# RWKV-7 recurrence in a two-layer encoder: transitions formed ahead of the chain, scratch laid out by token tile, transfers merged and spread

## The chip, the cores and the metric

One core of a Trainium2 chip runs the whole program. The metric is the device time of one execution in microseconds (us); the program is timed as a whole. Engines: TensorE (PE; its weight loads are PEld), VectorE (DVE), ScalarE (ACT), GpSimd (POOL) and SyncE (SP), whose queue issues the DMAs named here. Each engine runs its own instructions in the order in which they stand.

## What is computed

A trunk of two layers on 1024 tokens of width 1024, in float32. Layer 0 is attention and an MLP, and the change leaves both alone. Layer 1 mixes tokens by an RWKV-7 recurrence with 16 heads of 64, once forward and once backward, and then has an MLP. What matters of it:

```
def rwkv7_scan(r, w, k, v, kk, a):
    def step(state, inp):
        r_t, w_t, k_t, v_t, kk_t, a_t = inp
        sa = jnp.einsum('bhvk,bhk->bhv', state, -kk_t)
        state = (state * w_t[:, :, None, :] + sa[..., None] * (kk_t * a_t)[:, :, None, :]
                 + v_t[..., None] * k_t[:, :, None, :])
        return state, jnp.einsum('bhvk,bhk->bhv', state, r_t)
...
    for d in range(2):
        ...
        o = rwkv7_scan(*ins)            # reversed in time for d == 1
        ...
        dir_out.append((group_norm(o, gn_w, gn_b) + bonus.reshape(nB, S, D)) * g.astype(F32))
    y = dir_out[0] + dir_out[1]
    return y.astype(h.dtype) @ w_o
```

## The kernel before

The program runs attention, its MLP, the RWKV projections (`rwkv_proj`), the recurrence (`rwkv_scan`), the output projection (`layer_out`) and the second MLP. A scheduler orders the instructions within what the code's order, the buffers and the data allow; `tc.high_priority` moves some forward, and `tc.issue_after` ties one behind another.

`rwkv_proj` makes r, k, v, the decays, the rates and the gates in pieces of 128 channels by 512 tokens, and writes them to scratch in DRAM: per group of four heads (256 channels, two pairs of heads) `dr.rk` (r and the normed key), `dr.v`, `dr.y` (the bonus) and `dr.g` (gates, one per direction), laid out as partition, pair, 1024 tokens; a piece is stored in runs of 2 KB. `dr.x` (decay sums, rates, keys) is laid out by tile already, with runs of about 512 bytes.

`rwkv_scan` cuts the sequence into chunks of 64 tokens. Its unit of work, a tile here, is 128 tokens (two chunks c) of four heads in both directions: 16 chunk problems. Four tiles make a batch; there are 8 batches, so 32 tiles G, and one step of the main loop per tile. Direction 1 walks the tokens backward, so tile e of a group pairs tokens e (forward) with tile 7 - e (backward). Per tile there are these generators:

- `prep` loads x and rk of each direction, raises the decays (ScalarE), forms scaled queries `zr` (VectorE, L1253 and L1255) and keys `bk` (VectorE L1260, POOL L1261), multiplies them on TensorE (L1267) to the intra-chunk matrices `af`, which ScalarE copies out (L1270) and POOL masks (L1271). TensorE transposes the keys (L1279), ScalarE copies them to `bn` (L1281). `bk` holds each head's half of the partitions with zeros in the other half, so TensorE always works on all 128 rows. The strictly triangular part goes to the scratch `nd`.
- `invert`, once a batch, loads `nd` as `nb`, inverts 32x32 blocks by 60 small VectorE operations (L1298, L1300), stores them to `xd` and loads them back into `af` and as `xt`. All these transfers stand together behind the last operation.
- `post` loads v, centres it (L1339) into `sv`, and joins the inverted blocks (TensorE L1353, L1364, ScalarE copies L1357, L1367).
- `scan` walks the chain: for each of two chunks, two pairs of heads and two directions, TensorE adds what the state h gives to the chunk (L1389, L1393), ScalarE and VectorE copy that to `y` (L1395, L1396), TensorE applies the inverse (L1398), both engines copy to `sv` (L1400, L1401), TensorE forms the state's increment (L1404), VectorE the new state (L1413, with ScalarE's decayed old one, L1387), and TensorE the output (L1419, L1424), which ScalarE copies out to `ot` (L1427). Behind each of these eight visits `side()` advances the other generators by one piece.
- `finish` norms the output (TensorE L1446, two matmul records per tile, counted below to find steps), gates it, adds the bonus (POOL L1456) and stores to `yh`, or with the second half of the sequence to `yd`, which the output projection reads (L748).

Nine slots hold prepared tiles, so `prep` runs eight tiles ahead of the chain. Four chains of state are open at a time (two pairs, two directions), and a chunk of one of them needs the state of its predecessor.

Of the kernel before, what the change touches and what calls it, by code (L numbers as in the profile page):

```python
# [842 lines left out]
def rwkv_proj(tc, g, ap, ru, dr):  # L843
# [6 lines left out]
    with ExitStack() as es:  # L850
# [83 lines left out]
        def quad(x, pr, half):  # L934
            return x[pr // 2][:, pr % 2, ..., fsl(half, 512)] if len(x[0].shape) == 3 else x[pr // 2][:, pr % 2, :, fsl(half, 512)]

        def r_done(half):
            def done(pr, ps):
                o = po.tile([P, 512], F32, tag="o", name="o")
                nc.scalar.activation(o, ps, AF.Copy)  # L940
                nc.sync.dma_start(out=quad(dr.rk, pr, half)[:, 0], in_=o)

            return done
# [10 lines left out]
        def v_done(half):  # L954
            def done(pr, ps):
                y = po.tile([P, 512], F32, tag="y", name="y")
                nc.sync.dma_start(out=y, in_=quad(yb, pr, half))
                o = po.tile([P, 512], F32, tag="o", name="o")
                nc.scalar.activation(o, ps, AF.Copy)
                nc.sync.dma_start(out=quad(dr.v, pr, half), in_=o)  # L960
                nc.gpsimd.tensor_tensor(out=y, in0=y, in1=o, op=ALU.mult)
                nc.sync.dma_start(out=quad(dr.y, pr, half), in_=y)
# [44 lines left out]
        class Side:  # L1007
# [22 lines left out]
            def norm(self, nh, pr):  # L1030
# [18 lines left out]
                nc.sync.dma_start(out=quad(dr.rk, pr, nh)[:, 1], in_=kk)  # L1049

            def unit(self, w, nh, pr, d):
# [5 lines left out]
                if d == 0:  # L1057
# [3 lines left out]
                    nc.sync.dma_start(out=w.r, in_=quad(dr.rk, pr, nh)[:, 0])  # L1061
# [29 lines left out]
                nc.sync.dma_start(out=quad(dr.g[d], pr, nh), in_=o)  # L1091
# [11 lines left out]
                if d == 1:  # L1103
                    nc.gpsimd.tensor_tensor(out=w.y, in0=w.y, in1=kr, op=ALU.add)
                    nc.sync.dma_start(out=quad(yb, pr, nh), in_=w.y)
# [39 lines left out]
def rwkv_scan(tc, g, ap, dr, yd):  # L1145
# [3 lines left out]

    nc = tc.nc  # L1150
    NS = T // P
    NX = 4 * (65 + 2 * RC)
    with ExitStack() as es:
# [13 lines left out]
        hp = pool("s_h", 3)  # L1167
# [3 lines left out]
        t1 = pool("s_1", 1, "left")  # L1171
        te = pool("s_e", 2, "left")
        ip = pool("s_i", 1, "left")
        slots("left", 0, 1, 2, 8)
        psC = pool("s_pc", 1, space=PSUM)
        psA = pool("s_pa", 2, space=PSUM)
        psB = pool("s_pb", 1, space=PSUM)
# [8 lines left out]
        nc.vector.memset(gneps, GN_EPS)  # L1186

        dp = es.enter_context(tc.tile_pool(name="s_d", bufs=2, space=DRAM))


        hbd = [[t1.tile([P, P], F32, name=f"h{d}{i}") for i in range(2)] for d in range(4)]
        ybd = [t1.tile([P, 2, RC], F32, name=f"y{d}") for d in range(4)]
        for x in sum(hbd, ybd):
            nc.gpsimd.memset(x, 0.0)
        bk = t1.tile([P, 4, 2, 2, RC], F32, name="bk")
        for j in range(2):
            nc.gpsimd.memset(bk[fsl(1 - j, 64), :, j], 0.0)
# [4 lines left out]
        def psb():  # L1202
            return psB.tile([P, 512], F32, tag="B", name="B", bufs=1)

        def psl():
            return psB.tile([P, 512], F32, tag="L", name="L", bufs=1)
# [4 lines left out]
        def tokens(d, e, n):  # L1211

            return slice(e * P, (e + n) * P) if d == 0 else slice((NS - e - n) * P, (NS - e) * P)
# [5 lines left out]
        def quad(x):  # L1219
            return x.rearrange("p (q c) t -> p q c t", q=2)  # L1220

# [10 lines left out]
        def prep(q, i):  # L1232
# [4 lines left out]
            w.af = sp.tile([P, 2, 4, 2, P], F32, tag="af", name="af")  # L1237
            w.zr, w.bn = ([sp.tile([P, 4, 2, RC], F32, tag=f"{n}{d}", name=f"{n}{d}") for d in range(2)] for n in ("zr", "bn"))
            w.pc = [sp.tile([P, 4], F32, tag=f"pc{d}", name=f"pc{d}") for d in range(2)]
            for d in range(2):  # L1240
                x = te.tile([P, NX], F32, tag="x", name="x")
                nc.sync.dma_start(out=x, in_=dr.x[d][q.m][:, e, :])
                rk = te.tile([P, 2, 2, P], F32, tag="rk", name="rk")
                nc.sync.dma_start(out=rk, in_=dr.rk[q.m][:, :, :, tokens(d, e, 1)])
# [3 lines left out]
                ipr = te.tile([P, 4, RC], F32, tag="ipr", name="ipr", bufs=1)  # L1248
                nc.scalar.activation(ipr, cs[:, :, 1:65], AF.Exp, scale=KAPPA)
                nc.scalar.activation(cs, cs, AF.Exp, scale=-KAPPA)  # L1250
                nc.gpsimd.tensor_copy(w.pc[d], cs[:, :, 64])
                zr = w.zr[d]
                nc.vector.tensor_tensor(out=quad(zr[:, :, 0]), in0=quad(cs[:, :, 0:64]), in1=ordered(rk[:, :, 1], d),  # L1253
                                        op=ALU.mult)
                nc.vector.tensor_tensor(out=quad(zr[:, :, 1]), in0=quad(cs[:, :, 1:65]), in1=ordered(rk[:, :, 0], d),  # L1255
                                        op=ALU.mult)

                for j in range(2):
                    rows = fsl(j, 64)
                    nc.vector.tensor_tensor(out=bk[rows, :, j, j], in0=kd[rows], in1=ipr[rows], op=ALU.mult)  # L1260
                    nc.gpsimd.tensor_tensor(out=bk[rows, :, j, 1 - j], in0=a[rows], in1=ipr[rows], op=ALU.mult)  # L1261
                yield

                for j in range(2):
                    ps = psa()
                    for u in range(4):
                        nc.tensor.matmul(ps[:, fsl(u, P)], lhsT=bk[:, u, j].rearrange("p a b -> p (a b)"),  # L1267
                                         rhs=zr[:, u].rearrange("p a b -> p (a b)"), start=True, stop=True)
                    o = w.af[:, d, :, j, :]
                    nc.scalar.activation(o, ps.rearrange("p (u t) -> p u t", t=P), AF.Copy)  # L1270
# [193 lines left out]
        class Bulk:  # L1464


            def __init__(self):
                self.l = []
# [233 lines left out]
```

## Time and profile before

| | us |
|---|---|
| three timed runs | 3662.55, 3665.97, 3673.72; median 3665.97 |
| the profiled execution | 3667.36 |
| its span | 3665.6 |
| first to last preparation product (L1267) | 1896.3 to 2706.5 |
| first to last output copy of the chain (L1427) | 2088.6 to 2863.0 |
| TensorE busy over the span | 3183.3 (87%) |
| VectorE, ScalarE, POOL busy | 2533.5, 1849.0, 1772.7 |

Times inside the execution count from the span's start. "Busy" is the time in which at least one instruction of the engine ran; the granted clock (PEclk) is the part of TensorE's full clock that it was given. In the groups, `128*64 128x64` is the part of TensorE's array in use (rows by columns) and the result; a matmul of 32-bit floats leaves two records, a transpose one; "idle before" names what the engine waited for ahead of the group. In the waits the columns are total us, times, and the longest.

### The profile page before, as it was taken

How to read it: one execution, taken by the hardware profiler on the slowest of the kernel's cores; microseconds unless marked ns; L12 is line 12 of the kernel's file. 1: busy time of each engine (PE TensorE's matmuls, PEld its weight loads, DVE VectorE, ACT ScalarE, POOL GpSimd, SP SyncE). 2: the span in 40 equal slices, each digit the busy share in tenths (PEclk: the TensorE clock that was granted, in tenths of full speed). 3: DMA queues.
4: the chain of work that ended last, by engine and by line, in shares of the span. 5: the costliest groups of instructions: out<-in, count | busy, mean ns of one | idle time of the engine just before them, and what ended most of it. 6: DMA issues, size and time to landing. Idle time of an engine off the chain costs nothing. (4 is left out here: it accounts for less than half of the span.)

```text
span 3665.6 us, 61287 instructions
## 1 busy us (share of the span) xinstructions
PE 3183.3 (87%) x22168; PEld 2592.9 (71%) x22168; DVE 2533.5 (69%) x4649; ACT 1849.0 (50%) x4244; POOL 1772.7 (48%) x1610
## 2 busy tenths in 40 slices
PE   7999998899999988888887687788777889999998
PEld 6788887688777766665566566666666768877776
DVE  3355564654499978966954778887776474449996
ACT  2366564455543337754433365565566445554333
POOL 1000001565598884354666344444431156558887
PEclk9999999899999998999986687788887889999999
DMA  6222215233231133258775354455444423223113
GB/s 202 72 79 81 67 55 176 84 128 115 75 126 50 66 113 111 92 177 230 229 226 157 92 129 111 106 128 124 114 100 132 129 78 141 109 70 138 37 79 115
DMA packets 425101, 425.70 MB, mean 116 GB/s; under 512 B 138668, under 2 KB 338476, under 8 KB 418653
## 3 DMA queue, kind: packets, MB, share of 16 engines
q1 hardware_dynamic: 423612, 417.58, 36.8%
q0 software_dynamic: 1184, 4.20, 0.4%
q8 instruction: 174, 2.85, 0.3%
q14 instruction: 131, 1.07, 0.1%
HBM read 290.83 MB, written 138.20 MB: 117 GB/s over the span
## 5 line engine op out<-in xcount | busy, mean ns | idle before, releaser
L101 PE MATMUL pm<-bhi,lo 128*128 128x512 f32 x840 | 332.7, 399 | 45.6 <-DVE lo L130 45.4
L130 DVE TENSOR_TENSOR lo<-x,hi 128x512 fp32r<-128x512 f32 x300 | 322.0, 1079 | 63.3 <-ACT hi L129 63.1
L129 ACT ACTIVATE hi<-x 128x512 fp32r<-128x512 f32 x300 | 189.2, 631 | 330.1 <-DVE x L127 128.9
L100 PE MATMUL pm<-blo,hi 128*128 128x512 f32 x840 | 331.5, 395 | 8.7 <-POOL blo L130 8.2
L99 PE MATMUL pm<-bhi,hi 128*128 128x512 f32 x840 | 320.9, 395 | 5.3 <-ACT bhi L129 5.3
L127 POOL TENSOR_TENSOR x<-w1r 128x512 f32<-128x512 f32 x160 | 214.5, 1344 | 201.6 <-DVE lo L130 178.2
L1271 POOL TENSOR_TENSOR af<-af,amask 128x512 f32<-128x512 f32 x128 | 164.6, 1291 | 146.1 <-ACT af L1270 103.8
L130 POOL TENSOR_TENSOR blo<-bx,bhi 128x512 fp32r<-128x512 f32 x138 | 222.8, 1615 | 25.3 <-ACT bhi L129 25.0
L1267 PE MATMUL A<-zr,bk 128*128 128x128 f32 x1024 | 187.5, 347 | 47.1 <-DVE bk L1260 36.1
L101 PEld LDWEIGHTS pm<-bhi,lo 128*128 128x128 f32 x840 | 158.3, 189 | 98.1 <-DVE lo L130 66.8
L905 POOL TENSOR_TENSOR wl<-wr,wh 128x512 fp32r<-128x512 f32 (+2 forms) x144 | 160.1, 1123 | 127.8 <-ACT wh L904 92.7
L127 POOL TENSOR_TENSOR bx<-w 128x512 f32<-128x512 f32 x140 | 215.9, 1544 | 9.5
L1267 PEld LDWEIGHTS A<-zr,bk 128*128 128x128 f32 x1024 | 166.5, 250 | 59.8 <-POOL bk L1261 22.1
L127 DVE TENSOR_TENSOR x<-h 128x512 f32<-128x512 f32 x140 | 195.9, 1410 | 5.3 <-ACT h L268 2.7
L100 PEld LDWEIGHTS pm<-blo,hi 128*128 128x128 f32 x840 | 158.8, 189 | 49.4 <-POOL blo L130 16.0
L99 PEld LDWEIGHTS pm<-bhi,hi 128*128 128x128 f32 x840 | 159.8, 191 | 39.0 <-ACT bhi L129 6.2
L99 PE MATMUL mm<-xmh,wh 128*128 128x512 f32 x384 | 166.6, 452 | 9.3 <-ACT wh L904 5.4
L1413 DVE SCALAR_TENSOR_TENSOR h<-c,pc,hd 64x64 f32<-64x64 f32 x448 | 127.0, 283 | 50.1 <-PE c L1404 30.6
L886 DVE SCALAR_TENSOR_TENSOR x<-u,mu,x 128x512 f32<-128x512 f32 x192 | 153.9, 834 | 9.2 <-ACT x L884 6.7
L1419 PE MATMUL c<-af,sv 128*64 128x64 f32 x1024 | 97.3, 274 | 72.3 <-DVE h L1413 65.4
L583 ACT ACTIVATE S<-S,mneg 128x256 f32<-128x256 f32 (+2 forms) x256 | 124.5, 499 | 67.8 <-DVE mneg L578 44.8
L335 DVE TENSOR_TENSOR acc<-acc,pm 128x512 f32<-128x512 f32 x256 | 158.1, 675 | 0.0
(369 smaller groups left out, 9951.2 us busy)
## 6 DMA issues: line engine op xcount, KB each, us to landing
w1r<-in_mlp_w_dram SPq DMA_DIRECT2D x32, 1024.0 KB, 5.5
w<-in_mlp_w_dram SPq DMA_DIRECT2D x32, 1024.0 KB, 5.4
x<-x SPq DMA_DIRECT2D x64, 386.0 KB, 3.3
hd<-h SPq DMA_DIRECT2D x24, 1024.0 KB, 4.2
h<-hd SPq DMA_DIRECT2D x24, 1024.0 KB, 7.8
wr<-in_w_rkv_dram SPq DMA_DIRECT2D x96, 256.0 KB, 2.7
rk<-rk SPq DMA_DIRECT2D x64, 256.0 KB, 3.9
x<-cs SPq DMA_DIRECT2D x32, 260.0 KB, 4.2
```

The lines of the kernel that those rows point to most:

```text
L99: nc.tensor.matmul(out, lhsT=ahi, rhs=bhi, start=start, stop=False)
L100: nc.tensor.matmul(out, lhsT=ahi, rhs=blo, start=False, stop=False)
L101: nc.tensor.matmul(out, lhsT=alo, rhs=bhi, start=False, stop=stop)
L127: add.tensor_tensor(out=y, in0=x, in1=blocks[term[2]], op=ALU.add if term[1] == "+" else ALU.subtract)
L129: nc.scalar.activation(hi, x, AF.Copy)
L130: sub.tensor_tensor(out=lo, in0=x, in1=hi, op=ALU.subtract)
L335: dve.tensor_tensor(out=a, in0=a, in1=banks[j], op=ALU.add if sign == "+" else ALU.subtract)
L886: nc.vector.scalar_tensor_tensor(out=x, in0=at(2 * i), scalar=mu[:, i, c, kt:kt + 1], in1=x, op0=ALU.mult, op1=ALU.add)
L905: nc.gpsimd.tensor_tensor(out=wlo, in0=wr, in1=whi, op=ALU.subtract)
L1267: nc.tensor.matmul(ps[:, fsl(u, P)], lhsT=bk[:, u, j].rearrange("p a b -> p (a b)"), rhs=zr[:, u].rearrange("p a b -> p (a b)"), start=Tru ...
L1271: nc.gpsimd.tensor_tensor(out=o, in0=o, in1=consts["amask"].unsqueeze(1).to_broadcast([P, 4, P]), op=ALU.mult)
L1413: nc.vector.scalar_tensor_tensor(out=hn[rows, cols], in0=ch[rows, 128:192], scalar=pc[rows, u:u + 1], in1=hd[rows, cols], op0=ALU.mult, op ...
```

## The change

The chain is rewritten so that it holds only the state. A new generator `post_a` does what `post` did and also multiplies the centred values by the intra-chunk matrix (`y`, L1396 of the new code). A new generator `post_b` applies the inverse to the queries and to that product (L1420), and from the first result forms, per chunk, the transition of the state and the effective queries (TensorE L1431, VectorE L1435 and L1437, where `eye2` is the identity twice). It then starts the sums for the new state (`hb`) and the output (`ob`) in PSUM, with the parts that don't need the state (L1406, in the helper `sums`). `scan` adds to these sums what the state gives, once per chunk for all eight problems (two pairs of heads, two directions, two heads in the halves of the partitions), and multiplies by the decay (VectorE L1467).

In `prep` the keys hold one head per half of the partitions without zeros, in one operation each (VectorE L1273, POOL L1274), and TensorE's products (L1282) work on 64 rows at a time, in turn the upper and the lower; the transposes (L1295) take 128 rows, and there is a new one of `zr` (L1303). `sv` has no zeros left to set.

The scratch `rk`, `v`, `y`, `g`, `yh` and `yd` is laid out as partition, token tile, pair, 128 tokens. `both(x, e)` addresses the tiles of both directions at once, so `rk`, `v`, `y` and the results have one transfer per tile in place of two. The stores of `rwkv_proj`, and its reload of r, keep their piece of 512 tokens and are cut to runs of 512 bytes.

`invert` sets the blocks' diagonal on VectorE in place of POOL and issues its loads tile by tile over several pieces, its stores behind the latest loads and key copies (`mark`). The main loop has a written table of which generator advances at which of eight places of a step; loads are issued one step before their use.

The core of the diff:

```
-            w.af = sp.tile([P, 2, 4, 2, P], F32, tag="af", name="af")
+            xs = [te.tile([P, NX], F32, tag="x", name="x", bufs=3) for d in range(2)]
             for d in range(2):
-                rk = te.tile([P, 2, 2, P], F32, tag="rk", name="rk")
-                nc.sync.dma_start(out=rk, in_=dr.rk[q.m][:, :, :, tokens(d, e, 1)])
+                nc.sync.dma_start(out=xs[d], in_=dr.x[d][q.m][:, e, :])
+            rks = te.tile([P, 2, 4 * P], F32, tag="rk", name="rk")
+            mark["sp"] = nc.sync.dma_start(out=rks, in_=both(dr.rk[q.m], e))
+            yield
...
-                    nc.vector.tensor_tensor(out=bk[rows, :, j, j], in0=kd[rows], in1=ipr[rows], op=ALU.mult)
-                    nc.gpsimd.tensor_tensor(out=bk[rows, :, j, 1 - j], in0=a[rows], in1=ipr[rows], op=ALU.mult)
+                nc.vector.tensor_tensor(out=bk[:, :, 1:3], in0=quad(kd), in1=quad(ipr), op=ALU.mult)
+                nc.gpsimd.tensor_tensor(out=bk[:, :, 0:4:3], in0=quad(a), in1=quad(ipr), op=ALU.mult)
...
+                for u in range(4):
+                    for j in range(2):
+                        rows = fsl(j, 64)
+                        nc.tensor.matmul(ps[j][:, fsl(u % 2 * 2 + u // 2, P)], lhsT=bku[rows, u], rhs=zr[rows, u // 2, :, u % 2, :],
+                                         start=True, stop=True)
...
+        def post_b(q, i):
...
+            for ps, rhs in ((pw, lambda un: zrd[:, un // 2, 0, un % 2]), (pu, lambda un: w.y[:, un])):
+                for un, n, j in UNITS:
+                    for c in range(2):
+                        rows = fsl(c, 64)
+                        nc.tensor.matmul(ps[rows, fsl(un, RC)], lhsT=af[rows, c, un, 0:64], rhs=rhs(un)[rows],
+                                         start=True, stop=True)
...
+            for un, n, j in UNITS:
+                for c in range(2):
+                    rows = fsl(c, 64)
+                    nc.tensor.matmul(pm[c][fsl(j, 64), fsl(n, P)], lhsT=wt[rows, un], rhs=af[rows, c, un, 64:AFX],
+                                     start=True, stop=True)
+            for c in range(2):
+                pv = pm[c].rearrange("p (n t) -> p n t", t=P)
+                nc.vector.tensor_tensor(out=zrd[:, :, 0, c, :], in0=pv[:, :, 64:P],
+                                        in1=eye2.unsqueeze(1).to_broadcast([P, 4, 64]), op=ALU.add)
+                nc.vector.tensor_tensor(out=zrd[:, :, 1, c, :], in0=pv[:, :, 0:64], in1=zrd[:, :, 1, c, :], op=ALU.add)
...
+        def scan(q, i, hs):
...
+                        if h is not None:
+                            sums(w.fh[c], [(j, w.hb[c][fsl(j, 64), fsl(n, RC)], zrd[fsl(j, 64), n, 0, c, :],
+                                               h[fsl(j, 64), n, :]) for un, n, j in UNITS], True)
+                        hs[0] = hp.tile([P, 4, RC], F32, tag="h", name="h")
+                        nc.vector.tensor_tensor(out=hs[0], in0=c64(w.hb[c][:, 0:256]),
+                                                in1=w.pc.rearrange("p d u -> p (d u)")[:, c::2].unsqueeze(2).to_broadcast([P, 4, RC]),
+                                                op=ALU.mult)
...
-        dr.rk, dr.v, dr.y = quad("rk", 2, 2, T), quad("v", 2, T), quad("y", 2, T)
+        dr.rk, dr.v, dr.y = quad("rk", TT, 4, P), quad("v", TT, 2, P), quad("y", TT, 2, P)
```

How the order moves. TensorE before, in the middle of a step: `c` are the PSUM tiles of the four open chains, `h`, `zr`, `bn`, `y` and `sv` their operands.

```order
L1398 MATMUL c_23653<-y_17544,af 64x64 x2
L1389 MATMUL c_23734<-sv,af 64x64 x2
L1393 MATMUL c_23734<-h_17539,zr_20717 64x64 x2
L1404 MATMUL c_23587<-sv,bn_20366 64x64 x2
L1339 MATMUL B<-center,vr 64x64 x8
L1404 MATMUL c_23616<-sv,bn_20367 64x64 x2
L1404 MATMUL c_23653<-sv,bn_20718 64x64 x2
L1419 MATMUL c_23587<-af,sv 64x64 x2
L1424 MATMUL c_23587<-zr_20364,h_17540 64x64 x2
```

Each visit of a chain is a handful of pairs of matmuls, and each of `y`, `sv` and `h` comes from a copy on another engine between them.

TensorE of the change, across the two visits of the state in a step: `h_19634` and `h_19635` are the PSUM sums of the two chunks, `h` is the state.

```order
L1406 MATMUL h_19634<-h,zr 64x64 x6
L1303 MATMUL A<-ident,zr 128x128 x4
L1406 MATMUL o<-zr,h 64x64 x8
L1387 MATMUL B<-af,qs 32x32
L1396 MATMUL B<-sv,af 64x64 x3
L1387 MATMUL B<-af,qs 32x32 x15
L1396 MATMUL B<-sv,af 64x64 x13
L1406 MATMUL h_19635<-h,zr 64x64 x8
L1420 MATMUL B<-zr,af 64x64
L1406 MATMUL o<-zr,h 64x64
L1420 MATMUL B<-zr,af 64x64 x15
```

Between the two visits there are 44 matmuls of other tiles and of the output, and the next step's inverse (L1420) follows directly.

POOL before, in the run-up ahead of the first step: `bk` is the one buffer of keys, `af` the matrices that it masks, `pc` the decays.

```order
L1271 TENSOR_TENSOR af_17745<-af_17745,amask_17528 128x4x128
L1251 COPY pc1_17751<-x_17792 128x4
L1261 TENSOR_TENSOR bk_17560<-x_17792,ipr_17796 64x4x64
L1271 TENSOR_TENSOR af_17745<-af_17745,amask_17528 128x4x128
L1261 TENSOR_TENSOR bk_17560<-x_17792,ipr_17796 64x4x64
```

POOL of the change at the same place:

```order
L1289 TENSOR_TENSOR af_17947<-af_17947,amask_17525 128x4x128 x2
L1274 TENSOR_TENSOR bk_17985<-x_17773,ipr_17979 128x2x2x64
L1289 TENSOR_TENSOR af_17947<-af_17947,amask_17525 128x4x128 x2
L1274 TENSOR_TENSOR bk_18031<-x_17941,ipr_18025 128x2x2x64
```

Before, key halves and masks of two directions alternate; now one key operation stands behind both masks of the direction before it.

More of the change, by code (lines that the diff above doesn't have):

```diff
@@ L1186, in rwkv_scan @@
         nc.vector.memset(gneps, GN_EPS)
+        eye2 = cp.tile([P, 64], F32, name="eye2")
+        nc.gpsimd.tensor_tensor(out=eye2, in0=g.ident[:, 0:64], in1=g.ident[:, 64:128], op=ALU.add)
         dp = es.enter_context(tc.tile_pool(name="s_d", bufs=2, space=DRAM))
[L1191 to L1197, printed above, removed]
         def psa():
@@ L1262, in prep @@
[L1262 to L1270, printed above, removed]
+                bk = te.tile([P, 2, 4, RC], F32, tag="bk", name="bk", bufs=1)
@@ new lines, in invert @@
+            with tc.issue_after(mark["sp"].ins), tc.issue_after(mark["act"].ins):
+                nc.sync.dma_start(out=q.xd[0:2].rearrange("i j u s t -> (i j u) s t"), in_=nb)
+                for th in range(2):
+                    xbt = ip.tile([P, 512], F32, tag="xtmp", name="xbt")[0:64].rearrange("p (t s) -> p t s", s=32)
+                    nc.scalar.activation(xbt, nb[0:64, :, fsl(th, 16)].transpose([0, 2, 1]), AF.Copy)
+                    nc.sync.dma_start(out=q.xd[2].rearrange("j u t s -> (j u) t s")[:, fsl(th, 16)], in_=xbt)
@@ new lines, in scan @@
+                h = hs[0]
+                with tc.high_priority(50):
+                    if not (w.last and c == 1):
+                        if h is not None:
[5 more added lines that the diff above has]
+                                                op=ALU.mult)
@@ new lines, in scan @@
+                if h is not None:
+                    sums(w.fo, [(j, w.ob[fsl(j, 64), fsl(2 * n + c, RC)], h[fsl(j, 64), n, :],
+                                       zrd[fsl(j, 64), n, 1, c, :]) for un, n, j in UNITS], c == 1)
+                yield
+            ot = w.ot.rearrange("p d q c t -> p d q (c t)")
+            for d in range(2):
+                o = ot[:, places(4 * q.half + i).index(d)]
+                nc.scalar.activation(o if d == 0 else o[:, :, ::-1], w.ob[:, fsl(d, 256)].rearrange("p (q t) -> p q t", t=P), AF.Copy)
@@ L1507, in rwkv_scan, with of, run @@
-        hs = None
-        for G in range(4 * NB):
+        yh = [dp.tile([P, NS, 2, P], F32, name=f"yh{i}", bufs=1) for i in range(2)]
+        NB = KT
+        NG = 4 * NB
+        bs = {}
+        def of(f, G):
+            b = G // 4
+            if G >= NG:
+                return iter(())
+            if b not in bs:
+                bs[b] = Batch(b)
+            return f(bs[b], G % 4)
+        def run(x, n=None):
+            while n is None or n > 0:
+                if next(x, x) is x:
+                    return
+                n = n and n - 1
@@ new lines, in rwkv_scan, with begin @@
+        mark = {}
+        def begin(f, G):
+            x = of(f, G)
+            run(x, 1)
+            return x
+        p = begin(prep, 0)
+        for G in range(NQ - 1):
+            pn = begin(prep, G + 1)
+            run(p)
+            p = pn
+            if G == 3:
+                run(invert(bs[0]))
+        pa = begin(post_a, 0)
+        for G in range(2):
+            pan = begin(post_a, G + 1)
+            run(pa)
+            pa = pan
+            if G == 0:
+                run(of(post_b, 0))
@@ L1549, in rwkv @@
+            for x in (s, pb, p, pa, fin):
+                run(x)
+            p, pa = pn, pan
+            fin = finish(q, i)
+        run(fin)
 def rwkv(tc, g, ap, es_u, ru, h_in, layer_out):
```

398 lines of the change are left out of this document (176 added, 222 removed).

## The prediction, made before the change was run

> **What bounds the kernel now.** I read the page first, then busy time by stage, the waits inside the recurrence, the groups by shape there, TensorE's timeline, and the DMA landings. The profiled execution took 3667.4 us (span 3665.6), 1.4 us above the median of the three timed runs, so the sum below is made against 3667.4.
>
> ```profile
> span 3665.6 us, 61287 instructions
> core 0: us, PE busy (x) PEld busy (x) DVE busy (x) ACT busy (x) POOL busy (x), PEclk, DMA share, GB/s
> 1575.00:1885.00 310.00, 254.31 (x1157) 182.04 (x1156) 222.86 (x280) 140.37 (x244) 165.45 (x151) 0.92 0.73 215
> 1953.00:2084.00 131.00, 83.79 (x528) 74.73 (x528) 87.79 (x134) 49.87 (x116) 76.13 (x89) 0.60 0.49 121
> 2084.00:2707.00 623.00, 494.83 (x7758) 404.96 (x7760) 503.02 (x1362) 365.05 (x1218) 262.27 (x325) 0.81 0.46 115
> 2707.00:2871.00 164.00, 129.41 (x2296) 101.07 (x2293) 105.97 (x358) 100.60 (x344) 22.86 (x32) 0.76 0.42 119
> ```
>
> The rows are the projection that writes the scratch, the run-up (preparation of the first eight tiles), the 24 recurrence steps that also prepare a later tile, and the 8 that don't. The change edits these stages alone, 918 us from 1953 to 2871 plus the stores of the first. A full step lasts 623 / 24 = 26.0 us: TensorE busy 20.6 at a granted clock of 0.81, which is 16.7 us at full clock; VectorE busy 21.0, ScalarE 15.2. A light step lasts 164 / 8 = 20.5. No engine is full, so the waits come next (2084 to 2707):
>
> ```profile
> ACT hd L1387 <- DVE h L1413: 84.1, 85, 4.1
> PE c L1419 <- DVE h L1413: 57.2, 59, 4.3
> PE c L1398 <- DVE y L1396: 27.9, 27, 3.6
> PE c L1404 <- ACT sv L1401: 19.3, 21, 2.8
> ```
>
> TensorE's waits for the chain's own copies (state h, y, sv) are 104.4 us, 4.35 a step of its 5.4 idle. The chain and the loaded VectorE bound the step; TensorE's work is the floor under it.
>
> **The change, part by part.** *VectorE and ScalarE in a step.*
>
> ```profile
> L1413 DVE SCALAR_TENSOR_TENSOR h<-c,pc,hd 64x64 f32<-64x64 f32 x336 | 95.2, 283 | 39.3 <-PE c L1404 24.4 <-ACT y L1395 3.1 <-PE c L1393 2.6
> L1260 DVE TENSOR_TENSOR bk<-x,ipr 64x256 f32<-64x256 f32 x90 | 68.9, 766 | 5.9 <-PE A L1279 2.5 <-ACT y L1395 1.6
> L1396 DVE COPY y<-c 64x64 f32<-64x64 f32 x186 | 40.1, 226 | 10.4 <-ACT y L1395 7.9
> L1400 DVE COPY sv<-c 64x64 f32<-64x64 f32 x184 | 40.0, 226 | 30.7 <-PE c L1398 27.9
> L335 DVE TENSOR_TENSOR acc<-acc,pm 128x512 f32<-128x512 f32 x256 | 158.1, 675 | 0.0
> L1387 ACT ACTIVATE hd<-h,pc 128x128 f32<-128x128 f32 x168 | 66.7, 399 | 92.5 <-DVE h L1413 84.1 <-DVE h L1410 6.8
> L1427 ACT ACTIVATE ot<-c 128x64 f32<-128x64 f32 x186 | 39.4, 216 | 10.2 <-PE c L1424 8.3 <-PE c L1419 0.3 <-PE c L1398 0.2
> L1395 ACT ACTIVATE y<-c 64x64 f32<-64x64 f32 x186 | 37.8, 211 | 17.8 <-PE c L1393 15.9
> L1401 ACT ACTIVATE sv<-c 64x64 f32<-64x64 f32 x184 | 37.6, 212 | 70.1 <-DVE sv L1400 69.4
> L1281 ACT ACTIVATE bn<-A 128x256 f32<-128x256 f32 x90 | 32.8, 373 | 5.3 <-PE A L1279 5.0
> L1342 ACT ACTIVATE sv<-B 64x512 f32<-64x512 f32 x47 | 27.7, 589 | 0.7 <-PE c L1419 0.2
> L1446 PE MATMUL L<-osq,ones 128*128 128x512 f32 x46 | 36.5, 888 | 0.0
> ```
>
> VectorE loses L1413, L1396 and L1400 (175.3 / 24 = 7.3 us a step) and half of the key products L1260, now one instruction over 128 partitions instead of two over 64 (1.4). It gains six operations of 128x256 from PSUM, two for the state and four for the transitions. None of that shape is in the trace; between 283 ns (64 columns) and 675 (512), by columns, I take 0.45: 2.7 us. The inversion's memset that comes from POOL costs next to nothing. VectorE: 21.0 - 8.7 + 2.7 = 15.0. ScalarE loses the first five ACT rows (214.3 / 24 = 8.9) and gains seven 512-column copies at 0.59, two of 256 at 0.37 and two tiny exponentials at 0.2: 5.3 in all, leaving 11.6. POOL only loses work (memsets, decay copies, half of the key products). So after the change TensorE is the fullest engine.
>
> *TensorE in a step.* A matmul leaves two records, a transpose one. Start-to-start times at full clock:
>
> ```profile
> 2304.93 1.16 PE L1267 MATMUL A<-zr,bk 128*128 128x128 f32 x8
> 2306.02 0.34 PE L1389 MATMUL c<-sv,af 128*64 128x64 f32 x4
> 2306.18 0.29 PE L1404 MATMUL c<-sv,bn 128*64 128x64 f32 x4
> 2306.30 0.29 PE L1398 MATMUL c<-y,af 128*64 128x64 f32 x4
> 2306.42 0.29 PE L1393 MATMUL c<-h,zr 128*64 128x64 f32 x4
> 2306.53 0.40 PE L1339 MATMUL B<-center,vr 128*64 128x64 f32 x8
> 2306.87 0.46 PE L1279 MATMUL A<-ident,bk 64*128 64x64 f32 x4
> 2307.26 0.39 PE L1339 MATMUL B<-center,vr 128*64 128x64 f32 x5
> 2317.58 1.07 PE L1364 MATMUL B<-af,qs 32*32 32x32 f32 x32
> ```
>
> A full 128x128 record takes 1.09 / 8 = 136 ns; a 64-column one whose output alternates between the column halves 0.35 / 12 = 29 (from 2306.18 to 2306.53), although four of them span 0.29, so the halves run side by side; the centring 43 (0.34 / 8); a 64x128 transpose 98 (0.39 / 4); a 32x32 record some 31 (1.07 / 32 is 33, with the end of the last one in it). Priced so, the old step is 32 x 136 + 16 x 98 + 32 x 43 + 64 x 31 + 192 x 29 ns, plus 1.3 for the norm's product (36.5 x 0.81 / 23) = 16.2 us against 16.7 measured; I scale by 1.03.
>
> The new step: intra-chunk products on half the rows (L1282) 32 records, between 68 (two at once) and 136: 80, since adjacent records use different rows, gives 2.6 us; transposes 12 x 136 = 1.6; centring 16 x 86 = 1.4; 32x32 work 64 x 31 = 2.0; 96 records of 64x64 (L1396, L1420) between 29 and 58: 33, near the 32x32 row that also alternates both halves, 3.2; the transitions (L1431) 32 with 128 columns, between 58 and 116: 65, 2.1; state and output sums (L1406) 64 x 29 + 64 x 31 (to 58) = 3.9; norm 1.3. Sum 18.1, scaled 18.6; ends 17.4 and 26.4. So TensorE's work rises by 1.9 us; what falls is its waiting. Two state visits a step remain, one VectorE multiply each, with other tiles' work between them on TensorE, so I keep 0.8 us idle. At a busy share well above 0.9 I take a granted clock of 0.92, as in the projection row. Full step: 18.6 / 0.92 + 0.8 = 21.0. A light step lacks L1282 and the transposes (4.3 scaled): 14.3 at 0.87 (between the projection's clock and 0.81) = 16.4, + 0.6 = 17.0. Gains: 24 x 5.0 = 119 and 8 x 3.5 = 28.
>
> The Trainium skill (TensorEngine Tiling (Array Packing), Key Properties) says that changing the tiling mode, not just the tile, drains TensorE. Counted in the order of its instructions, a new step changes its array form about 23 times, an old one about 15. Nothing of a drain is plain in the rows, so they do not bear the rule out: at 2306.53 eight centring records, then four of another form, then centring again follow with at most 0.1 us extra.
>
> *Run-up.* Per direction, once the projection's work is gone:
>
> ```profile
> 1974.05 3.75 PE L1267 MATMUL A<-zr,bk 128*128 128x128 f32 x16 [1.80 <-DVE bk L1260]
> 1976.87 1.27 POOL L1271 TENSOR_TENSOR af<-af,amask 128x512 f32<-128x512 f32 x1 [2.38 <-ACT af L1270]
> 1980.63 0.79 POOL L1261 TENSOR_TENSOR bk<-x,ipr 64x256 f32<-64x256 f32 x1
> 1983.79 1.26 POOL L1271 TENSOR_TENSOR af<-af,amask 128x512 f32<-128x512 f32 x1 [2.37 <-issue]
> ```
>
> The period is 1983.79 - 1976.87 = 6.9. In the new order POOL holds key product, then both masks, strictly in turn: 0.8 + TensorE at the low clock of 0.60 (1.9 if halves overlap, 3.75 if not) + two ScalarE copies 1.2 + masks 2.5 + some 0.3 of hand-overs = 6.7 to 8.6. Taking 7.2, fifteen directions from 1953 end at 2061, with about 13 us of the first tile's inverse and transitions behind them: 2074 instead of 2084, a gain of 10 (ends +26 and -5).
>
> *Scratch by tile and merged loads.*
>
> ```profile
> x<-an SPq DMA_DIRECT2D x32, 256.0 KB, 4.3
> rk<-kk SPq DMA_DIRECT2D x16, 256.0 KB, 3.7
> v<-o SPq DMA_DIRECT2D x16, 256.0 KB, 3.2
> rk<-rk SPq DMA_DIRECT2D x64, 256.0 KB, 3.9
> ```
>
> The recurrence now issues one load for both directions of rk, v and y, in longer runs; its DMA share of 0.46 had room, so I count nothing (if that cover were gone, 4 us per tile would show as a wait for x or rk). A merged load waits until the buffers of both directions are free; behind it in SP's queue stand the next tile's x, v and gates, asked for a step ahead, and with three x buffers for two loads a tile one is always free. The projection's stores of rk, v, y and g (and its reload of r) go from 2 KB to 512 B runs, the runs that x<-an has already: 4.3 against 3.2 to 3.7 us. They are hidden stores, but that stage's DMA share is 0.73 and v's stores end just ahead of the run-up: -3 (0 to -15). The spread of the inversion's transfers moves issues in SP's queue behind the next tile's loads (issue order only): nothing, since a slot's inverse is asked for a step later.
>
> Sum: 3667.4 - 119 - 28 - 10 + 3 = 3513.
>
> **Rivals.** (a) Half-array tiles overlap fully and the clock rises: 17.4 / 0.96 + 0.3 = 18.4 and 13.5 / 0.92 + 0.3 = 15.0 a step, so 24 x 7.6 + 8 x 5.5 + 7 = 233: 3434. For it: the column halves' 29 ns. Against: rows that mix forms cost 43. (b) A new ping-pong: inverse, its copies, y, wt, transitions and sv cross between TensorE and ScalarE six times a step in fixed order, and two buffers serve eight PSUM tiles of preparation; the clock stays at 0.85 and 2.6 us idle remain: 24.5 and 19, so 48 + 5: 3614. Against: ScalarE falls to 11.6 of 21. (c) Each of 8 further form changes costs some 0.2 us, what a lone record lasts (0.29 - 3 x 0.029): 1.7 x 32 = 55 more, 3568. (The drain that the Trainium skill states, TensorEngine Tiling, Key Properties, would act this way.) (d) Slower: half-row tiles don't run side by side. Then work is 26.4, the step 26.4 / 0.95 + 0.5 = 28.3, the light one 20.2 / 0.9 + 0.5 = 22.9, and 24 x 2.3 + 8 x 2.4 = 74 is lost, less 5: 3736. It decides above 24.2 us of TensorE work. For it: the 98 ns of L1279, which used half the rows without alternating. (e) The waits only move and nothing comes of it: 3667.
>
> **How the numbers follow.** Forecast 0.45 (its own range 3470 to 3550), (a) 0.18, (b) 0.13, (c) 0.10, (d) 0.09, (e) 0.05. The range 3425 to 3620 takes in (a), (b) and (c) and leaves out (d), (e) and some 0.05 below. Faster by over 0.3% (11 us, about what a measurement tells from no change) 0.86, within 0.05, slower 0.09.
>
> **What would show it.** Steps of about 21 us between the norm's products, 17 in the last eight; granted clock above 0.9 there; VectorE near 15 us a step; no wait over a microsecond or two of TensorE on h; L1282 at 70 to 90 ns a record, L1420 at 30 to 35; the first state product near 2074. Wrong if L1282 stands at 136 or L1420 near 58, or if TensorE waits for ScalarE by several us a step.

## The result, and the profile after

The changed kernel takes 3717.2 us (median of four runs, 3697.6 to 3724.6) against 3664.6 for the kernel before in the same session: ratio 1.0129, 95% interval 1.0109 to 1.0149. It is 1.3% slower; 3513 was predicted, in a range of 3425 to 3620. Two executions below, one of e3 and one of the kernel before, took nearly twice as long as the others and are left out. The profiled execution of the changed kernel took 3719.5 us, span 3717.7, which is 52.1 more than the span before.

Busy time by stage of the changed kernel, in the columns of the prediction's first table (run-up; the 24 full steps; the light ones):

```profile
core 0: us, PE busy (x) PEld busy (x) DVE busy (x) ACT busy (x) POOL busy (x), PEclk, DMA share, GB/s
...
1953.00:2083.00 130.00, 64.73 (x622) 53.45 (x622) 49.68 (x111) 51.36 (x112) 51.34 (x47) 0.53 0.43 109
2083.00:2767.00 684.00, 538.35 (x8902) 454.42 (x8902) 295.89 (x738) 317.34 (x673) 197.70 (x189) 0.75 0.40 106
2767.00:2910.00 143.00, 114.32 (x2395) 93.72 (x2394) 60.16 (x145) 66.46 (x123) 15.22 (x17) 0.82 0.43 127
```

The full steps last 684 us in place of 623, which is 28.5 a step. That is where the time went: +61 there, -1 at the run-up's end (2083 for 2084), -11 in the light steps (from their start to the first product of the output projection: 145.2 for 156.3), +3 behind. TensorE worked 538.35 x 0.75 = 404 us at full clock in the full steps, and before 494.83 x 0.81 = 401: about the same work. (A product of two means is rough: for e6, e7 and e8 below, with the same matmuls as the changed kernel, it gives 388, 424 and 397.) Its idle time rose from 128 to 146 us and its clock fell from 0.81 to 0.75. So 18 of the 61 us are idle time, and the other 43 are busy time, most of it the same work at a lower clock. VectorE was busy only 12.3 us a step, ScalarE 13.2 and POOL 8.2. No engine is full, so the waits of this stage come next (total us, times, longest):

```profile
POOL vr L1359 <- DMA v<-v: 285.5, 20, 23.9
...
PE A L1282 <- DVE bk L1273: 65.6, 6, 14.4
...
POOL vr L1359 <- PE B L1431: 67.0, 5, 15.2
...
PE A L1282 <- POOL bk L1274: 44.1, 17, 10.2
...
PE B L1420 <- ACT af L1391: 26.5, 5, 9.2
```

TensorE no longer waits for the chain: for `h` it waits 0.2 us in all. It waits for keys: 65.6 us for VectorE's half of `bk`, in six waits (one a batch), and 44.1 for POOL's half, in seventeen. These are 110 of its 146 idle us. POOL in turn stood 285.5 us ahead of the copy `vr`, which reverses v, until the load of v landed; behind that copy in POOL's queue stand the masks and the next key.

One of the six long waits: TensorE's rows, then VectorE's with one of POOL (start, duration, idle before):

```profile
2539.95 1.12 PE L1496 MATMUL A<-osq,ones 128*128 128x512 f32 x2
2541.00 0.92 PE L1406 MATMUL h<-sv,af 128*64 128x64 f32 x24
2555.61 2.04 PE L1282 MATMUL A<-zr,bk 64*128 64x128 f32 x8 [13.70 <-DVE bk L1273]
...
2580.45 1.02 PE L1496 MATMUL A<-osq,ones 128*128 128x512 f32 x2
```

```profile
2542.33 0.20 DVE L1319 TENSOR_TENSOR xtmp<-nb 128x30 f32<-128x30 f32 x1 [9.46 <-DMA nb<-nd]
...
2546.22 1.25 DVE L1319 TENSOR_TENSOR xtmp<-nb 128x150 f32<-128x150 f32 x1
...
2548.26 0.33 DVE L1319 TENSOR_TENSOR xtmp<-nb 128x168 f32<-128x168 f32 x1
...
2555.05 0.42 DVE L1273 TENSOR_TENSOR bk<-x,ipr 128x256 f32<-128x256 f32 x1
2544.72 2.58 POOL L1289 TENSOR_TENSOR af<-af,amask 128x512 f32<-128x512 f32 x2
```

From one norm product to the next this step takes 40.5 us. VectorE waited 9.5 us for the inversion's load `nb`, ran 26 of its operations and the four of the transitions, and only then reached the key for which TensorE had stopped at 2541.9. In VectorE's order 30 products of the inversion stand ahead of one key in the loop's first batch, and runs of 4 to 16 in the others; before, after the loop's first batch, at most 8.

And what such a stop costs afterwards (same columns as the first table):

```profile
2542.00:2555.00 13.00, 0.00 (x0) 0.00 (x0) 11.85 (x30) 0.00 (x0) 3.69 (x4) 0.62 0.10 40
2555.00:2560.00 5.00, 4.39 (x27) 4.08 (x28) 4.90 (x15) 3.05 (x6) 0.00 (x0) 0.50 0.25 79
...
2565.00:2570.00 5.00, 5.00 (x56) 3.68 (x56) 2.77 (x8) 0.65 (x2) 0.00 (x0) 0.50 0.66 175
2570.00:2574.50 4.50, 4.50 (x100) 4.44 (x96) 2.62 (x9) 2.07 (x5) 0.00 (x0) 0.50 0.02 5
2574.50:2580.00 5.50, 5.50 (x119) 4.90 (x115) 3.99 (x16) 4.33 (x11) 0.00 (x0) 0.88 0.51 168
```

The granted clock falls to 0.50 during the wait and stays there for 19 us of work behind it. Such a wait costs its own length and half of these 19 us again. Counted in windows of half a microsecond, the clock stood below 0.75 for 338 us of the full steps, before for 236. It did not fall more often than before: there are 26 such stretches of 13.0 us on average, and before there were 34 of 6.9.

### The profile page after: what moved, and what is told of

The parts are those of the page before. It is cut to its first block, busy times and chain, and to the rows that moved or that the text cites. A ratio compares the mean times of both kernels' runs of the same rounds, so it can differ in the third digit from the quotient of the medians.

```text
span 3717.7 us, 61571 instructions
## 1 busy us (share of the span) xinstructions
PE 3197.2 (86%) x23512; PEld 2611.9 (70%) x23512; DVE 2238.4 (60%) x3789; ACT 1768.4 (48%) x3476; POOL 1668.7 (45%) x1397
## 5 line engine op out<-in xcount | busy, mean ns | idle before, releaser
L1282 PE MATMUL A<-zr,bk 64*128 64x128 f32 x1024 | 144.5, 355 | 146.7 <-DVE bk L1273 76.3
L1282 PEld LDWEIGHTS A<-zr,bk 64*128 64x128 f32 x1024 | 120.8, 249 | 161.3 <-POOL bk L1274 78.1
L1359 POOL COPY vr<-v 128x256 f32<-128x256 f32 x32 | 13.3, 416 | 409.4 <-DMA v<-v 342.5
L100 PE MATMUL mm<-xml,wh 128*128 128x512 f32 x384 | 156.9, 409 | 0.4 <-DVE xml L891 0.4
```

The lines of the kernel that those rows point to most:

```text
L100: nc.tensor.matmul(out, lhsT=ahi, rhs=blo, start=False, stop=False)
L1282: nc.tensor.matmul(ps[j][:, fsl(u % 2 * 2 + u // 2, P)], lhsT=bku[rows, u], rhs=zr[rows, u // 2, :, u % 2, :], start=True, stop=True)
```

## The experiments

The theories: A, the inversion's operations stand ahead of key products in VectorE's queue. B, POOL waits for v at the reversal, and masks and keys wait behind it. C, one buffer of keys holds the ring of key, product, mask and transpose. D, the half-array products themselves cost the time. F, in TensorE's order the products of the two directions stand too close for that ring. (E, on the clock, stands with e9.) Ratios are to the kernel before in the same session, where it took 3664.6 to 3674.2 us. Gains below are the difference of the ratio to the changed kernel's 1.0129, times 3665 us; by the two intervals such a gain is good to some 10 us, and in e3 to 13.

**e1, few inversion operations.**

```
+                if t in (2, 30) or q.b == 0:
                     nc.vector.tensor_tensor(out=tv, ...)
                     nc.vector.tensor_tensor(out=nb[:, 0:t, t + 1:32], ...)
```

> The changed kernel without 56 of the 60 inversion operations on VectorE in each batch from the second on (loads, stores and block joins stay; results differ). Theory A (inversion operations stand ahead of the key products in VectorE's queue, TensorE waits for keys): the 65.6 us of TensorE's waits for VectorE's key go, and most of the 46 us step of the last batch shrinks to about 20: 3717 - 66 - 25 = 3626, 3600 to 3650. Theory B (POOL waits for v at its reversal, masks and keys queue behind): 3717 to 3700, since POOL's waits stay. Theory D (half-array products are the cost): 3717.

3685.1 us, ratio 1.0042 (1.0026 to 1.0057): 32 us gained, some third of what A gave. TensorE's waits for VectorE's key are gone from the rows, but those for POOL's have nearly doubled (2083 to 2730):

```profile
PE A L1282 <- POOL bk L1274: 85.7, 24, 10.7
```

A is real, and behind it the next wait took over a part. D, for which the time would have stayed at 3717, can't be the whole cost, since TensorE's work was left alone; it goes out with e8, which has the same products and is faster than the kernel before.

**e2, two buffers for v.**

```
-            xv = te.tile([P, 2, 2 * P], F32, tag="v", name="v", bufs=1)
+            xv = te.tile([P, 2, 2 * P], F32, tag="v", name="v", bufs=2)
```

> The changed kernel with two buffers for v in place of one, so that a load does not wait for the centring of the tile before. Theory B: TensorE's waits for POOL's key (44.1 us) and some of the clock lost with them go: 3717 - 45 to 60 = 3657 to 3672. Theory A: 3707 to 3717, since VectorE's order is the same. Theory D: 3717.

3684.9 us, 1.0040 (1.0022 to 1.0058): 33 us gained, less than B's 45 to 60, far more than A's 0 to 10. The waits that answer, POOL's first (2083 to 2730), then TensorE's (2083 to 2700):

```profile
POOL vr L1359 <- PE B L1363: 219.8, 25, 21.0
```

```profile
PE A L1282 <- DVE bk L1273: 57.6, 6, 13.9
PE A L1282 <- POOL bk L1274: 20.5, 15, 1.5
```

POOL now waits for the buffer of `vr`, which the centring of the tile before sets free, and no longer for that centring and a load behind it. That is early enough: the longest of TensorE's waits for POOL's key is 1.5 us in place of 10.2.

**e3, no reversal copy.**

```
-                if d == 1:
-                    vr = te.tile([P, 2, P], F32, tag="vr", name="vr", bufs=1)
-                    nc.gpsimd.tensor_copy(vr, x[:, :, ::-1])
-                    x = vr
```

> The changed kernel without POOL's copy that reverses v of direction 1 (the values of that direction stay unreversed; results differ), so POOL never waits for a load of v; TensorE waits for it itself, later in the step. Theory B: 3650 to 3670. Theory A: 3705 to 3717.

3704.9 us, 1.0088 (1.0057 to 1.0119): 15 us gained, little more than the error, near A and far from B's 47 to 67. TensorE's waits for POOL's key fell to 24.7 us as in e2, but those of this kernel's L1416 (L1420 in the changed kernel) for ScalarE's `af` rose to 38.8 from 26.5. Why this gained less than e2 was not followed further.

**e4, two buffers for the keys.**

```
-                bk = te.tile([P, 2, 4, RC], F32, tag="bk", name="bk", bufs=1)
+                bk = te.tile([P, 2, 4, RC], F32, tag="bk", name="bk", bufs=2)
```

> The changed kernel with two buffers for the keys in place of one: a direction's key products need not wait for the transposes of the direction before (VectorE's waits for them: 49.2 us). Theory C (the ring of key, product, mask and transpose through one buffer sets the step): 3717 - 40 to 60 = 3657 to 3677. Theory A: 3700 to 3717, because up to 30 of the inversion's products still stand between two keys. Theory B: 3710 to 3717.

3704.5 us, 1.0087 (1.0066 to 1.0108): 15 us gained, little more than the error. C fails as the bound: the keys came early and TensorE's product waited elsewhere.

```profile
PE A L1282 <- ACT osq L1498: 114.6, 22, 14.0
```

L1498 reads the norm's product, which has its PSUM buffer from the same pair as the products of preparation.

**e5, e1 and e2 together.** The edits are those two.

> The changed kernel with both edits of the first two experiments (56 of 60 inversion operations of a batch left out, results differ; two buffers for v). If theories A and B name separate waits, their gains add: 3717 - 33 - 33 = 3651, 3640 to 3660. If either only uncovers the other (one ring behind both), the time stays at 3675 to 3685. Still far above the 3513 predicted in either case, since the ring of keys and products (theory F) is left: TensorE's products of the two directions stand close together in its order.

3633.1 us, 0.9893 (0.9876 to 0.9909): 86 us gained, more than 32 + 33. So A and B are not one ring; they stand in part side by side, and with one of them gone the other still holds TensorE (in e1 its waits for POOL's key nearly doubled). With both gone the clock recovers as well: 0.83 over the full steps, in place of 0.75.

**e6, products half a step apart.**

```
-                run(p, 1)
+                if k in (0, 1, 2, 4, 6, 7):
+                    run(p, 1)
```

> The changed kernel with another table for preparation: the second direction's key, product and transposes advance at places 4, 6 and 7 of a step in place of 3, 4 and 5, so TensorE's products of the two directions stand half a step apart and not behind one another. Theory F (with the products some 3.5 us of TensorE work apart, the ring of product, copy, mask and key, 6.7 us and more in the run-up, makes TensorE wait in every step, and each wait drops the clock to half): TensorE's waits for POOL's key go, the granted clock rises from 0.75 to 0.80 or more, 3717 - 30 to 60 = 3657 to 3687. Theory B alone (v's load): the wait moves with the product, 3705 to 3725.

3657.2 us, 0.9951 (0.9935 to 0.9967): 65 us gained by the table alone. In the changed kernel TensorE had, from the end of one direction's products (2405.20 in the rows further down) to the start of its wait for the other's (2408.60), 3.4 us of work, while the ring took 8.5 us in the run-up. TensorE's waits for POOL's key fell from 44.1 us to 1.2, and the clock rose to 0.82. The full steps:

```profile
2083.00:2694.00 611.00, 472.78 (x9022) 390.69 (x9020) 314.54 (x745) 319.79 (x678) 199.94 (x189) 0.82 0.46 120
```

That the order of the products costs 65 us is shown, but not that it costs them by F's wait. TensorE's idle time is 138 us, hardly less than 146: waits for VectorE's key (39.5), ahead of the transposes (30.3), at L1387 (25.0) and at L1431 (24.2) took the place of the old ones. What fell is TensorE's busy time, 538 to 473 us for the same matmuls, with 222 us at low clock in place of 338. In the changed kernel nine stops, all at L1282, were followed by 17 to 20 us of unbroken work before the clock came back; here none by more than some 11. Why the clock returns sooner in this order is open.

**e7, the inversion spread, with two buffers for v.** The pieces get a table over five half steps, and each is tied behind the latest key.

```
+                mark["dve"] = nc.vector.tensor_tensor(out=bk[:, :, 1:3], ...)
...
+                with (tc.issue_after(mark["dve"].ins) if q.b else ExitStack()):
                     nc.vector.tensor_tensor(out=tv, ...)
...
+                run(gi, table.get((i, k), 0))
```

> The changed kernel with two buffers for v and the inversion's operations tied behind the latest key product and spread over five half steps, at most 12 products between two keys in place of up to 30 (the whole computation). Theory A: most of what leaving them out gave beside two buffers of v comes back without leaving anything out: 3685 - 15 to 30 = 3655 to 3670. If VectorE's load and not the order is what counts: 3680 to 3690.

3620.8 us, 0.9862 (0.9841 to 0.9884): 98 us gained, more than A gave, and at least as much as e5 with hardly any inversion in it (the intervals overlap). What stands first seems to matter at least as much as how much there is: in e5 the first of the four operations left still waits for `nb` ahead of a key (36.1 us in all); here it stands behind, and this wait is gone from the rows.

**e8, e7 with e6's table.**

> Two buffers for v, the inversion spread, and the two directions' products half a step apart (the whole computation). If A, B and F name separate waits: 3717 - 33 - 25 - 45 = 3614, 3590 to 3640, below the kernel before (3666). If they are one ring: about 3660.

3606.5 us, 0.9812 (0.9789 to 0.9836): 116 us gained, and faster than the kernel before. The three don't add in full (98 + 65). Of its full steps TensorE is idle for 99 us, and the clock is low for 160 us.

**e9, trains of small tiles.**

```
+            for r, n in ((128, 100), (64, 300), (32, 300), (128, 100)):
+                for k in range(12):
+                    nc.vector.tensor_copy(b, a)
+                    nc.vector.tensor_copy(a, b)
+                for k in range(n):
...
```

> The kernel before, followed by four trains of matmuls, each behind some 15 us in which only VectorE works: 100 of the full array, 300 of 64x64 tiles (two quadrants in turn), 300 of 32x32 tiles (two in turn), 100 of the full array. Its time is longer by the trains and not compared. Theory E (work in small tiles does not lift the granted clock): it returns to 1.0 some 3 to 7 us into a full-array train, but only after 17 us or never in the trains of 64x64 and 32x32. Without E (any busy TensorE lifts it): 3 to 10 us in all four.

The trains, and the clock around their starts (columns as in the stage table):

```profile
3681.63 24.00 PE L1702 MATMUL tp<-ta 128*128 128x128 f32 x200 [18.06 <-DVE ta L1699]
3716.30 20.37 PE L1705 MATMUL tp<-ta 64*64 64x64 f32 x600 [10.67 <-DVE ta L1699]
3747.36 14.45 PE L1709 MATMUL tp<-ta 32*32 32x32 f32 x526 [10.68 <-DVE ta L1699]
```

```profile
3681.00:3684.50 3.50, 2.87 (x13) 2.90 (x14) 0.92 (x3) 0.00 (x0) 0.00 (x0) 0.50 0.01 2
3684.50:3705.00 20.50, 20.50 (x185) 20.50 (x184) 0.00 (x0) 0.00 (x0) 0.00 (x0) 1.00 0.01 2
3716.50:3722.50 6.00, 6.00 (x120) 6.00 (x120) 0.21 (x1) 0.00 (x0) 0.00 (x0) 0.53 0.01 3
3722.50:3737.00 14.50, 14.17 (x486) 14.04 (x482) 0.28 (x1) 0.00 (x0) 0.00 (x0) 1.00 0.01 3
3747.50:3765.00 17.50, 16.54 (x600) 16.18 (x598) 0.74 (x3) 0.00 (x0) 0.00 (x0) 0.50 0.02 5
3775.00:3780.50 5.50, 5.38 (x26) 5.38 (x27) 0.07 (x1) 0.00 (x0) 0.00 (x0) 0.53 0.00 0
3780.50:3800.00 19.50, 19.50 (x176) 19.44 (x175) 0.00 (x0) 0.00 (x0) 0.00 (x0) 1.00 0.01 2
```

The full array has its clock back after 2.9 us and, in the last train, after 5.4; 64x64 tiles after some 6; 32x32 tiles not in 17 us. E holds for 32x32 tiles and fails for 64x64, with one train of each.

**e10, the layout alone.** The kernel before with scratch by tile, for example:

```
-                nc.sync.dma_start(out=quad(dr.v, pr, half), in_=o)
+                nc.sync.dma_start(out=quad(dr.v, pr, half), in_=by_tile(o))
...
-                nc.sync.dma_start(out=x, in_=dr.v[q.m][:, :, tokens(d, e, 1)])
+                nc.sync.dma_start(out=x, in_=dr.v[q.m][:, tile_of(d, e)])
```

> The kernel before with one part of the change alone: the scratch rk, v, y, g, yh and yd by token tile (its stores in runs of 512 bytes, its loads in longer ones), with the chain, the preparation and two loads per tile as before. The prediction counted 3 us of loss for it (0 to 15): 3667 to 3682, most likely 3670. If the layout is what made the change slower: 3700 or more; if it gains: below 3660.

3667.5 us, 0.9982 (0.9971 to 0.9993): 7 us faster (3 to 11) than the kernel before. The layout isn't what made the change slower.

**e11, the inversion also behind the transitions.**

```
-                nc.vector.tensor_tensor(out=zrd[:, :, 1, c, :], ...)
+                mark["dve"] = nc.vector.tensor_tensor(out=zrd[:, :, 1, c, :], ...)
```

> The version of e8 with the inversion's operations tied also behind the latest transition, so that the first of them, which waits for its load, does not stand ahead of transitions that TensorE's state sums need. Theory A: e8's 3606 - 5 to 15 = 3591 to 3601; if the rest of the wait is elsewhere: 3600 to 3612.

3605.3 us, 0.9817 (0.9795 to 0.9839), the same as e8. The wait it was aimed at was worth nothing that can be measured.

**e12, key transposes into the other PSUM pool.**

```
-                ps = psa()
+                ps = psb()
                 for u in range(4):
                     nc.tensor.transpose(ps[:, fsl(u % 2 * 2 + u // 2, P)], bku[:, u], g.ident)
```

> The version of e11 with the key transposes writing to the other pool of PSUM buffers (three) in place of the two that the products use. In e8 TensorE waited 38.3 us ahead of the transposes for ScalarE's copies of the products (18 times). If that is a buffer wait: 3590 - 15 to 30 = 3560 to 3580 with the clock regained; if the wait only moves to ScalarE's next copy: 3585 to 3600.

3582.0 us, 0.9746 (0.9724 to 0.9768): 23 us better than e11, and the best kernel here, 2.5% faster than before. It was a buffer wait for the most part: ahead of the transposes TensorE waited 29.2 us in e11 and 12.3 here. The clock did not rise (0.87 in e11, 0.85 here). The full steps of e7, e8 and e12, in this order, each row from its own trace:

```profile
2083.00:2675.00 592.00, 499.01 (x9034) 416.35 (x9032) 325.27 (x746) 320.22 (x681) 201.30 (x192) 0.85 0.47 124
```

```profile
2083.00:2643.00 560.00, 461.34 (x9006) 378.31 (x9007) 329.45 (x742) 316.60 (x674) 197.63 (x188) 0.86 0.50 130
```

```profile
2083.00:2624.00 541.00, 458.72 (x8858) 376.93 (x8852) 313.09 (x734) 311.01 (x664) 196.86 (x186) 0.85 0.50 133
```

24.7, 23.3 and 22.5 us a step with the change's own work, against 28.5 as it came and 26.0 before.

## Why the prediction was wrong, step by step

**TensorE's work (18.6 us a step): right in kind, too high.** Seven rows of a stretch at a granted clock of 1.00 give the prices:

```profile
2395.00:2406.00 11.00, 11.00 (x288) 9.86 (x284) 2.08 (x5) 8.09 (x20) 1.15 (x2) 1.00 0.59 173
```

```profile
2401.26 1.28 PE L1420 MATMUL B<-y,af 64*64 64x64 f32 x32
...
2402.48 0.66 PE L1363 MATMUL B<-center,v 128*64 128x128 f32 x8
...
2403.50 0.68 PE L1406 MATMUL o<-zr,h 64*64 64x64 f32 x14
...
2404.11 1.16 PE L1282 MATMUL A<-zr,bk 64*128 64x128 f32 x16
...
2405.20 1.10 PE L1431 MATMUL B<-af,wt 64*64 64x128 f32 x32
...
2406.24 0.66 PE L1295 MATMUL A<-ident,bk 128*128 128x128 f32 x4
...
2407.68 0.92 PE L1406 MATMUL h<-sv,af 128*64 128x64 f32 x24
```

From start to start, L1282 takes 1.09 / 16 = 68 ns a record (80 taken; 68 was the lower end), L1431 33 (65), L1420 38 (33), the sixteen records of the centring 64 (86). The step's work is 404 / 24 = 16.8 us, or 16.2 to 17.7 by e6 and e7. One reading was wrong: the 31 ns of a 32x32 record came from 2317.58, where the granted clock was 0.50, and not from full clock; at 1.00 it is 20 (the last row below, up to 2123.04). Rival (d), half-row tiles not side by side, is out by the first of these prices.

Rival (c), a price for each change of the array's form, was right about the price and wrong about the number. Where the forms alternate at a clock of 1.00:

```profile
2119.00:2123.00 4.00, 4.00 (x92) 3.01 (x90) 2.19 (x4) 2.79 (x6) 2.26 (x3) 1.00 0.56 133
```

```profile
2120.00 0.33 PE L1303 MATMUL A<-ident,zr 128*128 128x128 f32 x1
2120.26 0.32 PE L1406 MATMUL h<-h,zr 64*64 64x64 f32 x2
2120.52 0.33 PE L1303 MATMUL A<-ident,zr 128*128 128x128 f32 x1
...
2122.41 0.69 PE L1387 MATMUL B<-af,qs 32*32 32x32 f32 x32
```

each group starts 0.26 us after the other, while inside longer groups a transpose takes 0.12 us (0.49 / 4 from 2406.24 to 2406.73) and two 64x64 records 0.08 to 0.09 (2403.50 to 2404.11). So a change costs some 0.15 us here. The Trainium skill's rule (TensorEngine Tiling (Array Packing), Key Properties) of a drain at a change of mode would act this way, and these rows agree with it, though they don't show that a drain is what takes the time. But in the order of the traces' records the changed kernel changes form 517 times in its 24 full steps (21.5 a step) and the kernel before 514 times. There is next to no further change to pay for, where the prediction counted eight a step.

VectorE's new operations were priced well (0.42 us for the state, 0.45 taken), and those that stayed ran shorter (`zr` 424 ns in place of 664); ScalarE came to 13.2 us a step where 11.6 was worked out.

**The terms that failed: "I keep 0.8 us idle" and "I take a granted clock of 0.92".** They were 6.1 us and 0.75. Against the predicted 21.0 x 24 = 504 us, the 684 come apart so: work -1.8 x 24 / 0.92 = -47; idle +5.3 x 24 = +126; clock 16.8 x 24 x (1 / 0.75 - 1 / 0.92) = +99; in all +178 of 180. The clock was taken from the projection's row because the busy share would be high. But the clock is 0.50 or 1.00 from moment to moment, and its mean follows from how often TensorE stops and how long each return takes, not from the share of its work. Here the returns took longer (13.0 us a stretch in place of 6.9), which the prediction had no term for.

**Why it was idle.** In three places the prediction put a cost at nothing.
- "The spread of inversion's transfers: nothing", and VectorE at 15.0 us a step. VectorE's mean was even less, 12.3, but the inversion's 60 operations fall into two of four steps, and a VectorE with less other work took them in closer runs ahead of the key (A; e1, e7). A mean over four steps hid the place.
- "A merged load waits until the buffers of both directions are free ... with three x buffers one is always free." The x buffers were not always free, and the one buffer of v was not thought of. SP's own waits in the full steps:

```profile
SPq L1248 <- DVE bk L1273: 125.7, 19, 17.7
...
SPq L1350 <- PE B L1363: 56.7, 15, 11.2
```

The load of x (L1248) stood 125.7 us for a key product to free a buffer, with the load of v (L1350) behind it, which then waited for its one buffer. It is this second wait that cost the time: the first is no shorter where v has two buffers (121.2 us in e2, 131.6 in the faster e8). "POOL only loses work" counted POOL's work and not what stands at the head of its queue (B; e2).
- The ring of key, products, copies, masks was worked out at 6.7 to 8.6 us for the run-up, and not asked of the step, where TensorE's order left 3.4 us between the two directions' products (F; e6). The order had shown it ahead of time. How it became time, by these waits or by the slower return of the clock behind them, is open (e6).

**The rivals.** (b) had the right form, idle time and a low clock from two-buffer rings, but put it on ScalarE and the wrong size: ScalarE's `af` at L1420 cost 26.5 us in all. With the three orders mended it comes to the front: in e8 TensorE's longest waits are for ScalarE's copies (42.1 us ahead of the transposes), and giving the transposes other PSUM buffers gained 23 us (e12). The slower rival (d) was the wrong one: what made the kernel slower is not the price of TensorE's products, since e8 has the same ones. None of the rivals let VectorE, POOL or SP hold up the preparation.

**Run-up (-10): -1.** Ten directions apart, two rows of POOL's masks:

```profile
1962.92 2.66 POOL L1289 TENSOR_TENSOR af<-af,amask 128x512 f32<-128x512 f32 x2 [4.75 <-ACT af L1285]
...
2047.87 2.67 POOL L1289 TENSOR_TENSOR af<-af,amask 128x512 f32<-128x512 f32 x2 [5.42 <-ACT af L1285]
```

84.95 / 10 = 8.5 us a direction, the upper end of 6.7 to 8.6, where 7.2 was taken (8.1 in the first seven, before an inversion's operation stands in between); 15 x 1.3 = 20 less than hoped, of which half was made good in the piece behind. **Light steps (-28): -11**, 18.2 us each. **Stores (+3): -7** with the layout alone (e10), the only part with the wrong sign, and too small to matter; e10 holds the longer loads as well as the stores. **The chain: right.** TensorE's waits for h are gone (57.2 us before), and with the three orders mended a step takes 23.3 us (e8), with the transposes' buffers moved 22.5 (e12), where 21.0 was predicted. The mechanism of the chain holds; what failed is the cover of the work that feeds it.

## What to carry to other kernels

An engine that executes in order passes on the wait at the head of its queue to everything behind: for each moved or added instruction that can wait for a load, list what stands behind it and who needs that, and don't take a low busy share for cover. Where TensorE needs two results of one ring in a step, put its two uses as far apart as the ring is long. Count a stop of TensorE as its own length plus half of the work at low clock that follows: here some 3 us a stretch before, 5 in the changed kernel, and up to 10 behind a long wait.

## What the runs showed of the hardware that was not expected

The granted clock takes two values, 0.50 and 1.00. Counted in windows of half a microsecond, the low stretches of the full steps last some 3.5, 7, 10, 13.5, 17, 20.5 us and so on up to 31, before, after and in e8: multiples of about 3.4. After a stop the clock came back in 2.9 and 5.4 us under full-array matmuls, in some 6 us under 64x64 tiles, and not at all in 17 us under 32x32 tiles (e9). With changes only every 3.4 us the first three don't differ; the last does. The Trainium skill (TensorE: Matmul & The Clock Gate, What's actually happening) gives two states and some 3.4 us of sustained work for the return; the trace agrees on the states, and roughly for the full array and 64x64 tiles, and not for 32x32 tiles. In the changed kernel nine returns took 17 to 20 us of unbroken work, in stretches that mix 32x32, 64x64 and full-array matmuls; before, none took more than some 9, and in e8 none more than some 10, though both run as many 32x32 matmuls. The 32x32 pieces can't be the whole reason: behind the long wait shown above 7.5 us of work on larger tiles (2555.61 to 2563.16) went by at 0.50 ahead of the first 32x32 record. The reason stays open.

VectorE's operations with two inputs in SBUF take about as long as one of POOL's while POOL works: in the rows of the long wait above, 1.25 us for 128x150 at 2546.22, during POOL's two masks of 1.29 us each (2544.72 to 2547.30), and 0.33 for the larger 128x168 at 2548.26. Their size hardly matters then: in e8 a 128x30 piece takes 1.26 us in POOL's work (at 2095.38) and 0.19 outside it. L1437, which reads one of its inputs from PSUM, takes 0.41 us either way. The Trainium skill (GPSIMD Engine Reference, Specifications) says that the two share interfaces to SBUF and contend when VectorE has two inputs there; the rows agree. How much of the inversion's delay this is was not measured apart.
